# A hybrid decoder block: mixers over pieces of 1,024 tokens, the input projection's feature tiles as seven-product pairs

## The chip, the cores and the metric

The kernel runs on one core of one Trainium2 chip. The metric is the time of one execution in microseconds (us). Engines are named as in the profile: PE multiplies matrices, PEld loads its weights, DVE is the vector engine, ACT the scalar engine (activations and copies), POOL is GpSimd, and SP issues the DMAs. PE writes into PSUM, which here has eight banks of 128 x 512 floats.

## The reference

One decoder layer on one sequence of 2,048 tokens with a model width of 1,024. What matters of it, per layer:

```
h = rms_norm(x) * (1 + scale) + shift
proj = h @ w_in           # q 512 | k,v 128 each | qm,km,vm,om 512 each | i,f 4 each | ga,gm 1024 each
y_a = sliding_window_attention(rope(q), rope(k), v, sinks)        # window 128
qm, km = silu(causal_conv4(qm, km))
y_m = sigmoid(om) * head_norm(mlstm(qm, km, vm, i, f))            # recurrent over chunks
merged = sigmoid(ga) * (y_a @ w_branch_attn) + sigmoid(gm) * (y_m @ w_branch_mlstm)
x = x + gate * rms_norm(merged @ w_out)
x = x + gate_f * rms_norm((silu(h2 @ w_gate) * (h2 @ w_up)) @ w_down)     # h2 from the new x; width 2816
```

Everything is float32. The kernel reaches float32 accuracy with fp32r matmuls: each operand is split into a rounded part `hi` and the rest `lo`, and a product takes three matmuls, hi x hi, hi x lo and lo x hi (`mm3`).

## The kernel before

**Two phases.** The mixers run over four blocks of 512 tokens, `block(b)`, one after the other. Then the FFN runs over two pieces of 1,024 tokens. A build-time planner lays out the order. `run` goes through a list of `Piece`s (mixers) and `run2` through a list of `Part`s (FFN): each is a weight tile with its split and its matmuls. Work beside them (attention, the mLSTM's chunks, the preparation of the next block's h) is written as generators, which `spawn` puts on a list with a due time; `tick`, called after every three matmuls, lets those that are due go a step, and `finish` drives some to their end. The due times count matmul time, in ns (`L_QK`, `L_KW`, `L_SOFT` and so on). The tile framework then orders the instructions of each engine by a modelled timeline and adds the waits and the buffers' reuse.

**One block.** h (8 tiles of 128 features x 512 tokens, hi and lo) lies in two tiles `hhi` and `hlo`. In this order: q, then k, v and the mLSTM's pre-gates, as token groups (`token_group`: tokens on the partitions, four PSUM banks at once); then attention is spawned (`stage2`) beside vm and the feature tiles of ga; then the feature tiles of qm and km (8) with convolution and SiLU in `evac_qk`, and of om (4); then the mLSTM's four chunks are spawned (`stage4`) beside the attention branch's tiles and the feature tiles of gm; then the mLSTM branch's tiles, and the output matmul with the residual (`residual_out`), beside which the next block's h is prepared (`hprep`).

A feature tile (`feature_tile`) is 128 output features x 512 tokens: 8 x 3 matmuls into one PSUM bank, emptied by its `evac`. Its weights are split once for each tile and block, 128 x 1024 at a time (lines 260 and 261). A block has 28: 8 of qm and km, 4 of om, 8 of ga and 8 of gm. All of a block's results (q, qm, km, vm, om, ga, gm, the branch inputs) stay in SBUF, in a pool of nine 1 MB tiles `big` and smaller ones `tm` and `tx`.

**The FFN's pairs.** Gate and up take two 128-feature tiles, two halves of the contraction and both 512-token halves of a piece as a 2 x 2 by 2 x 2 block product in the Strassen-Winograd form: seven products of 12 matmuls instead of eight. The table `PROD` names the operand of the weights and that of h (11, 21, 22 and the sums T1 to T4, in `HC`). `a_operands` makes the weight sums and splits, 128 x 512 each, four parts ahead; `pair_parts` gives the parts; `combine` adds up the results. Products 0, 2, 4 and 6 accumulate in one PSUM bank X, and what is in it is copied out after 0, 2 and 4:

```
if i == 0:
    R["P1"] = new()
    A.copy(R["P1"], ps)
elif i == 1:
    V.tensor_tensor(R["P1"], ps, R["P1"], op=ALU.add)
    done("11", R["P1"], False)
```

In the FFN X lies in one pool of four banks (`acc`) and the other products in a second pool of four (`mix`).

**Lines named in the prediction.** 205 issues every matmul and 210 every transpose. 1135 and 1136 split a 128 x 512 unit into hi (ACT) and lo (DVE). 1286 to 1288 and 1297 make a pair's weight sums. 1337 to 1351 are in `combine`. 912 to 918 are in `evac_qk`: the first convolution tap, the other three, the sigmoid, and the product. 926 scales om. 852 is attention's exponential, 856 its division on POOL.

## Time and profile before

| | |
|---|---|
| runs before | 2763.06 us median of 3 (2759.21 to 2763.97) |
| profiled execution | span 2761.2 us from the first to the last instruction; its own time outside the span is not shown |
| PE busy, matmuls and transposes | 2703.9 us (98%), 12654 |
| DVE / ACT busy | 1916.1 us (69%) / 1234.1 us (45%) |
| DMA | 402.64 MB, mean 146 GB/s |
| start, to 99.5 us | PE busy 73.09 of 99.50 |
| mixers, 99.5 to 1475 us | PE 1366.96, DVE 953.05, ACT 653.04 of 1375.50 |
| FFN, 1475 us to the end | PE 1263.89, DVE 885.20, ACT 534.26 of 1286.20 |

Busy time is the time in which an engine has at least one instruction under way. Matmuls overlap one another, so PE's busy share says where it stands still and not how fast it goes; the speed is read from how many matmuls start in a stretch. In the rows below, `out<-in` names the tiles an instruction writes and reads, `xN` is a count, and what stands behind the second bar is the engine's idle time just before these instructions and who ended it. The granted clock is the share of full speed that PE was allowed.

### The profile page before, as it was taken

The page shows a single profiled execution, that of the slowest core. Times are in us where ns is not written, and L with a number is a line of the kernel's source. Part 1 is how long each engine was busy: PE and PEld are TensorE (multiplying, and loading weights), DVE is VectorE, ACT ScalarE, POOL GpSimd, SP SyncE. Part 2 cuts the span into 40 slices and gives each one's busy share as a digit, 9 for nine tenths or more (in the row PEclk, how much of TensorE's full clock was granted, in tenths as well). Part 3 has the DMA queues.
Part 4 walks back from the last instruction along what each step waited for, and adds up shares of the span by engine and source line. Part 5 has one row for each costly group of instructions (what it writes and reads, how often), then busy time and mean ns, then how long its engine had stood idle before and what let it go on. Part 6 is the DMA issues. An engine that isn't in the chain of part 4 may idle for free.

```text
span 2761.2 us, 35099 instructions
## 1 busy us (share of the span) xinstructions
PE 2703.9 (98%) x12654; PEld 2198.3 (80%) x12654; DVE 1916.1 (69%) x3802; ACT 1234.1 (45%) x2285; POOL 149.6 (5%) x201
## 2 busy tenths in 40 slices
PE   6999999999999999999999999999999999999998
PEld 4778887788887888868887888887777888888886
DVE  7768667587674866747777777776676767666456
ACT  4543365434554335644363343334554333333444
POOL 2100000001000010110100000000000000000000
PEclk9999999999999999999999999999999999999999
DMA  7233353252442424423356555555676423334566
GB/s 235 89 111 97 101 205 105 80 135 83 167 166 66 136 86 153 167 67 101 94 183 212 174 179 167 176 161 192 207 237 206 133 96 111 98 108 136 185 213 214
DMA packets 280534, 402.64 MB, mean 146 GB/s; under 512 B 19220, under 2 KB 176536, under 8 KB 280360
## 3 DMA queue, kind: packets, MB, share of 16 engines
q1 hardware_dynamic: 280360, 400.40, 45.1%
q8 instruction: 99, 1.62, 0.2%
q14 instruction: 75, 0.61, 0.1%
HBM read 320.62 MB, written 79.73 MB: 145 GB/s over the span
## 4 chain that ended last, share of the span: by engine, by line
PE 52%; DVE 2%; DMA 2%; ACT 1%; issue 0%; POOL 0%; SPq 0%; DVEq 0%; POOLq 0%; ACTq 0%
PE acc L205 32%; PE mix L205 19%; DVE hl L1136 1%; DMA raw<-in_w_ffn_down_dram 1%; PE mix L210 1%; ACT hl L1135 0%; DMA raw<-as_d 0%; ACT big L1237 0%; DMA w<-hc_d 0%; DVE w L1497 0%; DMA raw<-in_w_ffn_gate_dram 0%; DMA ws_d<-big 0%; DVE big L1510 0%; DVE w L1533 0%; DVE w L1538 0%
## 5 line engine op out<-in xcount | busy, mean ns | idle before, releaser
L1135 ACT CAST hl<-raw 128x512 fp32r<-128x512 f32 x564 | 337.6, 621 | 403.2 <-PE mix L205 168.8
L1136 DVE TENSOR_TENSOR hl<-raw,hl 128x512 fp32r<-128x512 f32 x564 | 376.6, 686 | 170.7 <-ACT hl L1135 167.9
L260 ACT CAST whi<-raw 128x1024 fp32r<-128x1024 f32 (+1 forms) x208 | 212.2, 1020 | 499.9 <-PE acc L205 444.6
L261 DVE TENSOR_TENSOR wlo<-raw,whi 128x1024 fp32r<-128x1024 f32 (+1 forms) x208 | 249.0, 1197 | 177.5 <-ACT whi L260 175.2
L205 PE MATMUL acc<-hhi,wlo 128*128 128x512 f32 x896 | 356.9, 398 | 0.0
L205 PE MATMUL acc<-hhi,whi 128*128 128x512 f32 x896 | 353.8, 395 | 0.0
L205 PE MATMUL acc<-hlo,whi 128*128 128x512 f32 x896 | 352.9, 394 | 0.0
L205 PE MATMUL acc<-big,hl 128*128 128x512 f32 x1056 | 254.2, 389 | 0.7 <-ACT w L1343 0.7
L205 PE MATMUL acc<-hl,hl 128*128 128x512 f32 x1008 | 236.9, 393 | 7.2 <-DVE hl L1136 4.7
L205 PEld LDWEIGHTS acc<-big,hl 128*128 128x128 f32 x1056 | 198.0, 188 | 42.4 <-ACT w L1343 1.1
L205 PEld LDWEIGHTS acc<-hl,hl 128*128 128x128 f32 x1008 | 187.0, 188 | 52.9 <-DVE hl L1136 9.8
L205 PEld LDWEIGHTS acc<-hhi,whi 128*128 128x128 f32 x896 | 169.7, 189 | 41.2 <-issue 8.1
L205 PEld LDWEIGHTS acc<-hhi,wlo 128*128 128x128 f32 x896 | 169.5, 189 | 39.4 <-issue 4.1
L205 PEld LDWEIGHTS acc<-hlo,whi 128*128 128x128 f32 x896 | 169.3, 189 | 39.5 <-issue 4.9
L205 PE MATMUL mix<-big,hl 128*128 128x512 f32 x704 | 197.3, 391 | 2.6 <-DVE big L1272 2.6
L205 PE MATMUL mix<-hl,hl 128*128 128x512 f32 x792 | 182.4, 391 | 1.8 <-ACT hl L1135 1.0
L205 PEld LDWEIGHTS mix<-hl,hl 128*128 128x128 f32 x792 | 148.0, 188 | 35.5 <-DVE hl L1136 2.6
L205 PE MATMUL acc<-whi,big 128*128 128x512 f32 x512 | 166.5, 396 | 0.0
L205 PE MATMUL acc<-big,whi 128*128 128x512 f32 x512 | 158.4, 394 | 0.0
L205 PEld LDWEIGHTS mix<-big,hl 128*128 128x128 f32 x704 | 132.5, 189 | 30.5 <-DVE big L1272 3.0
L205 PE MATMUL acc<-whi,hhi 128*128 128x512 f32 (+1 forms) x384 | 133.1, 370 | 12.9 <-ACT hhi L505 9.1
L205 PE MATMUL acc<-wlo,hhi 128*128 128x512 f32 (+1 forms) x384 | 139.4, 367 | 2.1 <-DVE wlo L261 2.1
(336 smaller groups left out, 4725.3 us busy)
## 6 DMA issues: line engine op xcount, KB each, us to landing
raw<-in_w_in_dram SPq DMA_DIRECT2D x76, 1024.0 KB, 5.3
as_d<-w SPq DMA_DIRECT2D x154, 256.0 KB, 2.2
raw<-as_d SPq DMA_DIRECT2D x70, 512.0 KB, 3.7
raw<-in_w_ffn_gate_dram SPq DMA_DIRECT2D x22, 1024.0 KB, 5.5
raw<-in_w_ffn_up_dram SPq DMA_DIRECT2D x22, 1024.0 KB, 6.2
raw<-ws_d SPq DMA_DIRECT2D x40, 512.0 KB, 4.7
tx<-in_w_ada_dram SPq DMA_DIRECT2D x64, 256.0 KB, 3.6
raw<-in_w_out_dram SPq DMA_DIRECT2D x16, 1024.0 KB, 5.2
```

The lines of the kernel that those rows point to most:

```text
L205: T.matmul(o, lhsT=lhsT, rhs=rhs, start=start, stop=stop, skip_group_check=resumed)
L210: T.transpose(o, i, ident[:k, :k])
L260: A.copy(hv, src)
L261: V.tensor_tensor(lv, src, hv.bitcast(F32), op=ALU.subtract)
L1135: A.copy(v(hi), src)
L1136: V.tensor_tensor(v(lo), src, v(hi).bitcast(F32), op=ALU.subtract)
```

## The change

The two 512-token blocks of a 1,024-token piece are worked together (`superblock(sb)`), and the 28 feature tiles of each block become 14 pairs for each piece, with the FFN's `pair_parts`. The order in a piece is: q, k, v and the pre-gates of the first block; its attention is started; vm of both blocks; q, k, v of the second block; its attention is started; then the pairs; the mLSTM's eight chunks are started after the eighth pair; then the outputs of both blocks.

- h of the two blocks and its sums T1 to T4 (`HC`) take up to fourteen `big` tiles (the pool grows from nine to fourteen; `tx` from six to nine). `hprep` of the second block reads the first one's h back from DRAM, makes the four sums and writes them out; `hsums` reads and splits them.
- What a block hands on (q, qm and km, vm, om, the gates, the branch inputs) is written to DRAM and read back where it is used: by attention for each 128 queries, by the mLSTM for each chunk, by the outputs in 1 MB tiles.
- All seven products of these pairs use the four `acc` banks. The side work keeps the `mix` banks.
- Sigmoid is made from tanh in the mixers; the factors of two are folded into the constants. The convolution's first tap and om's scaling move from DVE to ACT. The post-mix gain `gg_m` lies in DRAM.
- `Piece` and `run` go; the mixers use `Part` and `run2`. A constant of the build, the DMA scratch size, is set to 1024.

The core of the diff:

```diff
-    bpool = ctx.enter_context(tc.tile_pool(name="bpool", bufs=9))
+    bpool = ctx.enter_context(tc.tile_pool(name="bpool", bufs=14))
...
+        for k in range(4):
+            v11, v21 = tx([P, 512]), tx([P, 512])
+            nc.sync.dma_start(v11, hv_d[sb][:, k, :])
+            nc.sync.dma_start(v21, hv_d[sb][:, k + 4, :])
+            v12 = one(k)
...
+            V.tensor_tensor(v11, v12, v11, op=ALU.subtract)
+            V.tensor_tensor(v12, v22, v12, op=ALU.subtract)
+            V.tensor_tensor(v22, v22, v11, op=ALU.subtract)
+            V.tensor_tensor(v21, v21, v22, op=ALU.subtract)
+            for i, v in enumerate((v11, v22, v12, v21)):
+                nc.sync.dma_start(ht_d[sb][:, i, k, :], v)
...
+    def hsums(sb, names):
+        for name in names:
+            for k in range(4):
+                v = tx([P, 512])
+                nc.sync.dma_start(v, ht_d[sb][:, int(name[1]) - 1, k, :])
+                split_unit(v, hc_part(name, 0)[:, k, :], hc_part(name, 1)[:, k, :])
+                yield L_HS
...
+            qth, qtl = ld([GQ, P], F32R), ld([GQ, P], F32R)
+            for i, q in enumerate((qth, qtl)):
+                nc.sync.dma_start(q.bitcast(F32), q_d[b][:, i, t, :].rearrange("p (j q) -> p j q", j=GQ))
+            yield 0
...
+            nc.sync.dma_start(km, qk_d[b][:, 1, :, cs])
...
+            nc.sync.dma_start(vc[:, :, :MD], vm_d[b][:, t, :].rearrange("p (h d) -> p h d", h=MH))
+            yield L_LOAD
...
+        def done_qk(p):
+            def done(qd, v, in_psum):
...
+                A.activation(ac, u[:, 0:TB], AF.Identity, scale=col("conv_w", f), bias=col("conv_b", f))
+                for j in range(1, 4):
+                    V.scalar_tensor_tensor(ac, u[:, j:j + TB], col("conv_w", j * 8 + f), ac, op0=ALU.mult, op1=ALU.add)
+                sg = tx([P, TB])
+                A.activation(sg, ac, AF.Tanh, scale=0.5)
+                V.scalar_tensor_tensor(ac, sg, 1.0, ac, op0=ALU.add, op1=ALU.mult)
+                nc.sync.dma_start(qk_d[b][:, f // 4, f % 4, :], ac)
...
+            return pair_parts(w_in, c0 + p * 256, done, new, plain, acc_tile)
...
+        def load_y(b, i0):
             for i in range(2):
-                A.activation(R["ga", i], R["ga", i], AF.Sigmoid)
-            R["ml"] = [spawn(mlstm(), L_ML)]
+                R["y", b, i0 + i] = big([4, TB], F32R)
+                nc.sync.dma_start(R["y", b, i0 + i].bitcast(F32), y_d[b][:, i0 + i, :, :])
...
+        pairs = [("qk", 0), ("om", 0), ("qk", 1), ("om", 1), ("qk", 2), ("ga", 0), ("qk", 3), ("ga", 1),
+                 ("ga", 2), ("ga", 3), ("gm", 0), ("gm", 1), ("gm", 2), ("gm", 3)]
+        for i, (kind, p) in enumerate(pairs):
+            parts = list(in_pair(kind, p))
...
+            if i + 1 == len(pairs):
+                yield from parts[:2]
+                yield lambda: (load_y(b0, 0), load_g(b0, 0))
+                parts = parts[2:]
+            yield from parts
+            if (kind, p) == ("ga", 1):
+                yield lambda: end_attention(b1)
+                yield lambda: spawn(mlstm(), L_ML)
+        yield from outputs(b0)
+        yield from outputs(b1)
```

## The prediction

> **What bounds the kernel now.** I read the page first, then the groups of instructions by line, the chain of waits in order of time, and last the busy time in windows. The page gives the span and the engines:

> ```profile
> span 2761.2 us, 35099 instructions
> PE 2703.9 (98%) x12654; PEld 2198.3 (80%) x12654; DVE 1916.1 (69%) x3802; ACT 1234.1 (45%) x2285; POOL 149.6 (5%) x201
> ```

> The three runs before took 2759.21 to 2763.97 us, median 2763.06. That is 1.9 us above the span of the profiled execution, whose own time outside the span is not shown. I make the sum in the span and add 1.9 at the end. A difference of 0.2% (5.5 us) is about what a measurement of this kernel can tell from none.

> PE is busy for 98%, but matmuls are pipelined: one lasts 395 ns and a new one starts sooner. What a matmul costs is therefore its spacing, and that is in the chain of waits (start, length, engine, count). The first row is the mixer, the second one product of the FFN's seven-product pairs:

> ```profile
> 1233.09 51.68 PE acc L205 x227
> ...
> 1575.40 2.72 PE mix L205 x12
> ```

> 51.68 / 227 = 0.2277 us and 2.72 / 12 = 0.2267 us: the two forms of product run at the same rate. I use 0.2267.

> The windows split the span into start, mixers and FFN (stretch, length, PE, PEld, DVE, ACT, POOL busy with counts, granted clock, DMA share, GB/s). The later rows are a stretch of gate/up pairs, then the first down projection:

> ```profile
> 99.50:1475.00 1375.50, 1366.96 (x6707) 1104.00 (x6706) 953.05 (x2131) 653.04 (x1221) 118.48 (x124) 1.00 0.39 121
> ...
> 1500.00:1850.00 350.00, 350.00 (x1544) 289.19 (x1543) 262.75 (x434) 132.86 (x244) 2.16 (x4) 1.00 0.53 174
> 1900.00:2125.00 225.00, 217.95 (x967) 176.01 (x966) 149.80 (x254) 121.84 (x230) 6.51 (x8) 1.00 0.66 220
> ```

> In the mixers PE stands still for 8.5 of 1375.5 us. So whatever PE no longer has to do there is a gain, as long as nothing else makes it wait. DVE is busy for 69% there, ACT for 47%.

> **What the change removes.** The feature tiles of qm/km, om, ga and gm are these groups (count | busy, mean ns):

> ```profile
> L205 PE MATMUL acc<-hhi,wlo 128*128 128x512 f32 x896 | 356.9, 398 | 0.0
> L205 PE MATMUL acc<-hhi,whi 128*128 128x512 f32 x896 | 353.8, 395 | 0.0
> L205 PE MATMUL acc<-hlo,whi 128*128 128x512 f32 x896 | 352.9, 394 | 0.0
> ```

> 3 x 896 = 2688 matmuls, that is 28 tiles x 24 x 4 blocks. After, there are 14 pairs in each of two pieces of 1,024 tokens, with 7 products of 12 matmuls: 14 x 2 x 84 = 2352. So 336 matmuls go, worth 336 x 0.2267 = 76.2 us, all of it in the stretch where PE is the path. Every other matmul and transpose keeps its count: queries, keys and v are still made block by block, and the branch and output matmuls are as before.

> **What it adds on DVE and ACT.** The FFN's pairs show each operation, and the mixer shows what goes:

> ```profile
> L1136 DVE TENSOR_TENSOR hl<-raw,hl 128x512 fp32r<-128x512 f32 x564 | 376.6, 686 | 170.7 <-ACT hl L1135 167.9
> L1135 ACT CAST hl<-raw 128x512 fp32r<-128x512 f32 x564 | 337.6, 621 | 403.2 <-PE mix L205 168.8 <-PE acc L205 161.9 <-DMA raw<-as_d 30.1
> L1287 DVE TENSOR_TENSOR raw<-raw 128x512 f32<-128x512 f32 x44 | 29.9, 680 | 0.0
> L1339 DVE TENSOR_TENSOR w<-mix,w 128x512 f32<-128x512 f32 x44 | 29.9, 680 | 0.1
> L261 DVE TENSOR_TENSOR wlo<-raw,whi 128x1024 fp32r<-128x1024 f32 (+1 forms) x208 | 249.0, 1197 | 177.5 <-ACT whi L260 175.2 <-PE mix L205 1.4
> L260 ACT CAST whi<-raw 128x1024 fp32r<-128x1024 f32 (+1 forms) x208 | 212.2, 1020 | 499.9 <-PE acc L205 444.6 <-issue 52.2 <-DVE big L714 2.8
> L912 DVE TENSOR_SCALAR tx<-tx,cols 128x512 f32<-128x512 f32 x32 | 17.3, 539 | 0.0
> L926 DVE TENSOR_SCALAR big<-big,cols 128x512 f32<-128x512 f32 x16 | 8.8, 547 | 0.2 <-ACT big L925 0.2
> ```

> DVE, for one pair: 7 splits (686 ns), 4 weight sums (680), 4 additions out of PSUM (680) = 10.2 us beside 84 x 0.2267 = 19.0 us of matmuls; 28 pairs make 287 us. Out go 112 splits of 1024 columns, 112 x 1.2 = 134, and the convolution's first tap and om's scaling, which move to ACT: 32 x 0.539 + 16 x 0.547 = 26. In come the sums of h and their splits, 32 x 0.680 + 32 x 0.686 = 44. Net +171 us. DVE in the mixers goes from 953 to about 1124 us, of 1375.5 - 76.2 = 1299: 87%. ACT: 196 x 0.621 - 112 x 1.020 = +7, the new splits of h 32 x 0.621 = 20, the moved scalings 48 at about 0.6 = 29, so 653 + 56 = 709, 55%. The evacuation copies stay at four a pair, and tanh takes sigmoid's place one for one.

> Neither sum is above PE's. I cost this work at nothing in itself, because the gate/up stretch above hides the same pair at DVE 75% (262.75 of 350) with PE at 350.00 of 350. A saturated DVE need not stop PE either. This is the mLSTM of the second block, where DVE worked without a pause:

> ```profile
> 610.00:640.00 30.00, 30.00 (x168) 25.89 (x168) 29.86 (x108) 6.50 (x8) 5.79 (x5) 1.00 0.30 89
> ```

> In the new order the chunks are eight in a row with a planned load time added, beside gate pairs that need only the 10.2 us. The heavier place is the qk pairs: each adds four convolutions on DVE and has attention of the second block beside it.

> **What it adds on the DMA queues.** A block's q, qk, v, om, gates and branch inputs are now written to DRAM and read back: 2 + 2 + 1 + 1 + 4 + 4 = 14 MB, twice, in four blocks 112 MB. The sums of h add 24 and gg_m 2.5; w_in's feature columns (14 MB) are read twice instead of four times, -28. Net +110 MB on 121 GB/s x 1375.5 us = 166 MB, so about 276 MB in 1.3 ms: 211 GB/s and, by the same share per byte, 0.68 of the engines. The first down projection is the nearest row to that (220 GB/s, 0.66, above). Two prices of a transfer (count, KB each, us to landing):

> ```profile
> raw<-in_w_in_dram SPq DMA_DIRECT2D x76, 1024.0 KB, 5.3
> as_d<-w SPq DMA_DIRECT2D x154, 256.0 KB, 2.2
> raw<-as_d SPq DMA_DIRECT2D x70, 512.0 KB, 3.7
> ```

> The tightest load is at the start of the outputs: two branch tiles and two gate tiles of 1 MB are loaded behind the second product of the last pair. The branch tiles land after 2 x 5.3 = 10.6 us and are needed after 5 x 2.72 = 13.6; the gates land at 21.2 and hold PE only when four PSUM banks are full, 13.6 + 4 x 2.72 = 24.5. That is 3.3 us of cover for the tanh of the gates, once for each piece; without cover it is a few us. Attention's query load is followed by its matmuls with no planned delay. Exposed, the 16 loads cost at most 16 x 3.7 = 59 us, hidden nothing. The order of PE's instructions is laid out at build time by modelled readiness, so other matmuls go ahead; I take hidden. All these transfers pass SP, where a write waits for its data, and behind it wait the weight loads, fetched a pair (19 us) ahead.

> **The waits that are new on PE.** A feature tile had four PSUM banks of 5.44 us each to be emptied. A pair accumulates products 0, 2, 4 and 6 in one bank: ACT must copy it before the product after next, one product (2.72 us) later. There are 84 such copies, and behind each waits everything in PE's order. The FFN shows this copy, and 1.0 us of PE's time in which it came late:

> ```profile
> L1337 ACT COPY w<-acc 128x512 f32<-128x512 f32 x44 | 25.6, 581 | 2.0 <-PE acc L205 2.0
> L205 PE MATMUL acc<-hcT2h,hl 128*128 128x512 f32 x352 | 116.0, 390 | 1.0 <-ACT w L1337 1.0
> ```

> A 0.58 us copy in a 2.72 us slot leaves 2.1 us for what ACT has in front of it. Bounds for the stalls: from below nothing (the gate/up row, PE 350.00 of 350), a little less if the waits around attention become fewer. From above the down row, where splits came late at 5.00 of 5 us of DVE:

> ```profile
> 1970.00:1975.00 5.00, 4.00 (x17) 2.85 (x16) 5.00 (x9) 4.77 (x10) 0.00 (x0) 1.00 0.87 235
> ```

> There PE lost 225 - 217.95 = 7.05 us, 3.1%. On the pairs and the attention and mLSTM beside them (28 x 19.0 us, plus about 200 us of side work: estimated) that is 0.031 x 732 = 23 us; on the whole mixer 0.031 x 1299 = 40 us. I take 23, because ACT and DMA come near that row only in these stages.

> A stall can cost more than itself. In the stretch from 460 to 470 us, beside attention and with DVE nearly full, PE lost 1.62 us and the granted clock fell afterwards:

> ```profile
> 460.00:470.00 10.00, 8.38 (x36) 6.52 (x35) 8.85 (x25) 2.58 (x8) 1.78 (x1) 0.83 0.25 63
> 464.00:466.00 2.00, 1.95 (x7) 1.73 (x8) 1.94 (x8) 0.00 (x0) 0.00 (x0) 0.57 0.00 0
> 466.00:468.00 2.00, 2.00 (x7) 1.53 (x6) 2.00 (x7) 0.00 (x0) 0.00 (x0) 0.58 0.27 32
> ```

> 14 matmuls in 4 us instead of 17.6: 0.8 us more, so such a stall costs some 2.4. [...]

> **The sum.** 2761.2 - 76.2 + 23 = 2708.0 us of span, and 1.9 more as a time: 2710 us.

> **The rivals.** First, the pairs run clean, as in gate/up: 2761.2 - 76.2 + 1.9 = 2687. For it speaks PE's 30.00 of 30 under a full DVE; against it, DVE at 87% over all and only four banks for a pair that in the FFN has eight.

> Second, contention over the whole mixer: 40 us instead of 23, and the query loads half exposed (30): 2757 at worst, 2727 without them. For it speaks the DMA share of 0.68; against it, that the loads are mostly placed far ahead.

> Third, slower: ACT stands still for the convolution. Its tanh waits for DVE's three taps, and the copy of the shared bank stands behind that tanh. The chain is these rows:

> ```profile
> L914 DVE SCALAR_TENSOR_TENSOR tx<-tx,cols,tx 128x512 f32<-128x512 f32 x96 | 72.0, 750 | 2.7
> L918 DVE SCALAR_TENSOR_TENSOR big<-tx,tx 128x512 f32<-128x512 f32 x32 | 21.9, 684 | 0.0
> L916 ACT ACTIVATE tx<-tx 128x512 f32<-128x512 f32 x32 | 20.1, 627 | 0.0
> ```

> Two outputs finish at the same product, so a tanh can stand behind a whole chain of 3 x 0.750 + 0.684 = 2.93 us. If each of the 32 outputs holds PE so long, that is 94 us: 2761.2 - 76.2 + 94 + 1.9 = 2781. It decides from 76.2 / 32 = 2.4 us an output. Against it: this tanh's sigmoid never made ACT idle before (0.0 in L916's row), as the order is laid out to fill such gaps. For it: the gaps were then filled under a DVE at 69%. [...]

> That the saving fails to appear as fewer matmuls I exclude: the counts are fixed in the program.

> **Chances.** The forecast 0.40, clean 0.19, contention 0.19, the convolution's chain 0.19, and 0.03 that stalls just cancel the saving. So faster 0.78, same 0.03, slower 0.19. The range runs from 2681 (clean, with the existing 8.5 us of idle mostly gone) to 2768 (contention at its worst with a few us more); it leaves out the chain.

> **What would show it.** PE should have 12318 matmuls, 84 in 19.0 us in a gate pair. DVE should read some 85% in the mixers, ACT 55%, DMA 0.68. PE's idle time in the mixers should be 20 to 35 us, mainly in the qk pairs, its releasers ACT's copies and splits. I am wrong if PE's idle time exceeds 76 us, if its wait is on a DMA rather than on ACT or DVE, or if the stretch before 100 us or the FFN changes by more than 5 us.

## The result, and the profile after

The kernel after took 2799.03 us (median of four runs, 2796.49 to 2799.59), the kernel before 2761.14 us beside it (four runs, 2759.02 to 2763.97). The ratio is 1.0133, with a 95% interval from 1.0118 to 1.0147. The change makes the kernel 38 us slower, where 51 us less was forecast.

The page of the kernel after begins:

```profile
span 2797.0 us, 35939 instructions
...
PE 2662.1 (95%) x12318; PEld 2153.6 (77%) x12318; DVE 2049.0 (73%) x4063; ACT 1259.2 (45%) x2430; POOL 161.7 (6%) x201
```

The matmuls fell to 12318, as counted in advance. Yet PE's busy time fell by only 41.8 us and the span grew by 35.8. To see where, I cut both traces into windows (stretch, length, PE, PEld, DVE, ACT, POOL busy with counts, granted clock, DMA share, GB/s). First the mixers of the kernel before, up to 2 us ahead of the FFN's first copy out of PSUM (in the kernel after, 3 us):

```profile
62.00:1469.00 1407.00, 1396.62 (x6912) 1129.81 (x6911) 979.67 (x2220) 671.26 (x1256) 118.85 (x127) 1.00 0.39 120
```

Then the kernel after, by stage. The first three rows are the first piece: q, k, v and vm; the four qk pairs with om, ga 0 and ga 1 among them, attention beside them; the other gate pairs with the mLSTM, and the outputs. The next three are the second piece, then come the FFN and the mixers as a whole:

```profile
62.00:231.00 169.00, 144.89 (x757) 112.62 (x756) 129.57 (x326) 86.70 (x211) 14.02 (x17) 0.92 0.62 202
231.00:430.00 199.00, 180.14 (x812) 136.75 (x811) 162.58 (x351) 99.53 (x223) 13.40 (x10) 0.97 0.37 119
430.00:790.00 360.00, 358.42 (x1751) 301.43 (x1750) 267.03 (x591) 172.19 (x294) 40.57 (x42) 1.00 0.70 235
790.00:948.00 158.00, 138.09 (x761) 108.46 (x761) 120.72 (x304) 81.57 (x202) 14.45 (x16) 0.94 0.64 209
948.00:1140.00 192.00, 174.51 (x787) 131.78 (x784) 158.36 (x328) 94.91 (x214) 11.88 (x10) 0.97 0.37 118
1140.00:1494.00 354.00, 349.01 (x1706) 292.85 (x1705) 271.67 (x593) 156.78 (x250) 36.10 (x33) 0.99 0.73 236
1494.00:2797.00 1303.00, 1277.64 (x5584) 1041.05 (x5582) 891.37 (x1461) 537.91 (x984) 16.02 (x21) 1.00 0.51 167
62.00:1494.00 1432.00, 1345.06 (x6562) 1083.88 (x6561) 1109.92 (x2487) 691.66 (x1392) 130.43 (x127) 0.97 0.60 197
```

PE stands still for 86.9 us of the mixers, where it stood still for 10.4 (1407.00 - 1396.62). Of the 86.9, the two q, k, v stretches have 24.1 + 19.9 = 44.0, the two stretches of qk pairs 18.9 + 17.5 = 36.4, and everything else 1.6 + 5.0. PE's busy time fell by 1396.62 - 1345.06 = 51.6 where the missing matmuls are worth 76.2, so 25 us are missing. Most of them are a lower clock, 0.92 to 0.97 in the four stretches with the idle time. In the trace the clock stands at 0.50 for 78.5 us of the mixers (10.2 before); PE is busy in 48.1 us of these (10.2 before) and loses half of that, 24.0 us (5.1 before). So 19 of the 25 us are the lower clock, and the other 6 are not explained. The mixers' account is -76 for the matmuls, +76 of idle time, +19 of lower clock and +6 open. The FFN counted from its first copy (1471.2 us before, 1497.2 after) takes 10 us more.

What PE waited for in the kernel after (engine, line waited for: us in all, times, longest us):

```profile
PE acc L206 <- ACT tx L751: 30.2, 7, 15.1
PE acc L206 <- ACT tx L1094: 11.5, 4, 4.1
PE acc L206 <- ACT big L521: 8.3, 3, 3.2
...
PE acc L206 <- DVE hl L1315: 7.0, 7, 2.9
PE mix L211 <- POOL tm L928: 6.6, 5, 2.6
PE mix L206 <- DVE big L1395: 6.1, 1, 6.1
...
PE acc L206 <- DVE tm L599: 4.4, 1, 4.4
```

Line 751 is the rotary's copy out of PSUM, line 1094 the copy of a qk pair's last result out of the shared bank. L521, which evacuates h, was there before (9.1 us in L505). So two places are new and large, and they lie in the two kinds of stretch that lost the time. They are not all of it: L751 has 30 of the 44 us in the q, k, v stretches, and L1094 only 11.4 of the 36.4 in the qk stretches, where the rest is spread over the pairs' splits, attention and the mLSTM.

**The first place: q, k, v.** This is the longest stall. ACT's timeline (start, length, engine, line, operation, and in brackets the idle time ahead of it and who ended it):

```profile
815.54 0.76 ACT L523 ACTIVATE tx<-mix,sh,s 128x512 f32<-128x512 f32 x1
823.83 0.27 ACT L751 COPY tx<-acc 128x128 f32<-128x128 f32 x1 [7.52 <-DMA ht_d<-tx]
```

SP's queue in the same stretch:

```profile
815.15 8.35 SPq L545 DMA_DIRECT2D ht_d<-tx x8
```

This row merges eight issues of 0.32 to 0.87 us, 3.3 us in all; between them SP waits, and at the end for sums that DVE makes late, because what it reads is late:

```profile
819.77 0.69 DVE L540 TENSOR_TENSOR tx<-tx,tx 128x512 f32<-128x512 f32 x1 [1.76 <-DMA tx<-hv_d]
```

The rotary's copy needs a free `tx` tile. Before the change it wrote a `tm` tile; now it shares nine `tx` tiles with `hprep`, which forms the sums of h in four of them at a time and holds them until they are written to DRAM. Reads and writes stand in a burst there:

```profile
806.00:812.00 6.00, 1.38 (x11) 0.84 (x9) 4.22 (x14) 5.98 (x12) 0.00 (x0) 0.77 1.05 399
812.00:818.00 6.00, 0.00 (x0) 0.00 (x0) 5.13 (x14) 4.27 (x6) 0.00 (x0) 0.50 1.02 351
818.00:824.00 6.00, 0.00 (x0) 0.00 (x0) 3.65 (x7) 0.17 (x1) 0.00 (x0) 0.50 1.05 383
824.00:828.00 4.00, 3.86 (x9) 3.12 (x10) 2.96 (x17) 0.89 (x4) 1.21 (x4) 0.50 0.66 250
```

The DMA share is over 1.0 for 18 us, at 350 to 400 GB/s, in a stage whose mean is 0.64. PE's own timeline shows what followed:

```profile
824.14 0.80 PE L206 MATMUL acc<-whi,big 128*128 128x512 f32 x1 [15.11 <-ACT tx L751]
```

It stood still for 15.1 us and then ran at half clock until 829.7 us: 9 matmuls in the 4 us from 824, where 17.6 go at full speed.

**The second place: the qk pairs.** ACT's timeline at one of the four waits:

```profile
334.02 0.63 ACT L1104 ACTIVATE tx<-tx 128x512 f32<-128x512 f32 x1 [1.42 <-DVE tx L1102]
334.56 0.57 ACT L1094 COPY tx<-acc 128x512 f32<-128x512 f32 x1
```

DVE's timeline ahead of it:

```profile
331.11 1.54 DVE L1102 SCALAR_TENSOR_TENSOR tx<-tx,cols,tx 128x512 f32<-128x512 f32 x2
332.64 0.69 DVE L1315 TENSOR_TENSOR hl<-raw,hl 128x512 fp32r<-128x512 f32 x1
333.25 0.74 DVE L1102 SCALAR_TENSOR_TENSOR tx<-tx,cols,tx 128x512 f32<-128x512 f32 x1
```

And PE's:

```profile
335.18 12.13 PE L206 MATMUL acc<-big,hl 128*128 128x512 f32 x45 [3.29 <-ACT tx L1094]
```

DVE makes the three taps with a split between them; ACT's tanh (L1104) waits for the third; the copy of the shared bank stands behind the tanh and starts only 0.54 us after it; PE waits for the copy. That is the third rival's chain, link by link, at this one place. All 32 tanh operations together, in the groups by line (count | busy, mean ns | idle before, releaser):

```profile
L1104 ACT ACTIVATE tx<-tx 128x512 f32<-128x512 f32 x32 | 20.2, 630 | 26.3 <-DVE tx L1102 26.2
```

26.2 us of ACT's idle time, where the same row of the kernel before (L916) had 0.0.

### The profile page after: what moved, and what is told of

The parts are those of the page before. It is cut to its first block, busy times and chain, and to the rows that moved or that the text cites. A ratio compares the mean times of both kernels' runs of the same rounds, so it can differ in the third digit from the quotient of the medians.

```text
span 2797.0 us, 35939 instructions
## 1 busy us (share of the span) xinstructions
PE 2662.1 (95%) x12318; PEld 2153.6 (77%) x12318; DVE 2049.0 (73%) x4063; ACT 1259.2 (45%) x2430; POOL 161.7 (6%) x201
## 4 chain that ended last, share of the span: by engine, by line
PE 78%; DVE 10%; DMA 7%; ACT 2%; issue 1%; SPq 0%; POOL 0%; DVEq 0%; POOLq 0%; ACTq 0%
PE acc L206 55%; PE mix L206 21%; DVE hl L1315 2%; PE mix L211 2%; DMA tx<-in_w_ada_dram 1%; DVE tx L1102 1%; DMA raw<-in_w_ffn_down_dram 1%; ACT hl L1314 1%; DMA ht_d<-tx 1%; DVE tm L431 1%; DMA raw<-as_d 1%; DMA q_d<-tx 1%; DMA tx<-in_g_post_ffn_dram 0%; DVE wlo L262 0%; DMA raw<-in_w_in_dram 0%
## 5 line engine op out<-in xcount | busy, mean ns | idle before, releaser
L206 PE MATMUL acc<-big,hl 128*128 128x512 f32 x3936 | 949.8, 396 | 24.0 <-ACT tx L1094 11.5
L206 PEld LDWEIGHTS acc<-big,hl 128*128 128x128 f32 x3936 | 737.8, 190 | 190.0 <-ACT tx L1094 13.2
L206 PE MATMUL acc<-whi,big 128*128 128x512 f32 (+1 forms) x1280 | 387.5, 382 | 39.4 <-ACT tx L751 30.2
L206 PE MATMUL mix<-big,hl 128*128 128x512 f32 x1232 | 332.9, 391 | 7.3 <-DVE big L1395 6.1
L206 PEld LDWEIGHTS acc<-whi,big 128*128 128x128 f32 x1280 | 237.4, 193 | 90.0 <-ACT tx L751 32.5
L206 PE MATMUL acc<-wlo,big 128*128 128x512 f32 (+1 forms) x640 | 242.3, 380 | 0.4 <-DVE wlo L262 0.4
L261 ACT CAST whi<-raw 128x1024 fp32r<-128x1024 f32 (+1 forms) x96 | 94.3, 982 | 131.7 <-PE acc L206 118.4
L262 DVE TENSOR_TENSOR wlo<-raw,whi 128x1024 fp32r<-128x1024 f32 (+1 forms) x96 | 109.7, 1145 | 58.8 <-ACT whi L261 54.2
L206 PEld LDWEIGHTS acc<-wlo,big 128*128 128x128 f32 x640 | 124.1, 194 | 23.9 <-issue 2.4
L206 PE MATMUL acc<-hcT2h,hl 128*128 128x512 f32 x352 | 118.1, 396 | 1.1 <-ACT w L1458 1.0
## 6 DMA issues: line engine op xcount, KB each, us to landing
raw<-in_w_in_dram SPq DMA_DIRECT2D x48, 1024.0 KB
as_d<-w SPq DMA_DIRECT2D x154, 256.0 KB
raw<-as_d SPq DMA_DIRECT2D x70, 512.0 KB
raw<-in_w_ffn_gate_dram SPq DMA_DIRECT2D x22, 1024.0 KB
raw<-in_w_ffn_up_dram SPq DMA_DIRECT2D x22, 1024.0 KB
raw<-ws_d SPq DMA_DIRECT2D x40, 512.0 KB
tx<-in_w_ada_dram SPq DMA_DIRECT2D x64, 256.0 KB
y_d<-tm SPq DMA_DIRECT2D x64, 256.0 KB
```

Source lines behind the costliest of these rows:

```text
L206: T.matmul(o, lhsT=lhsT, rhs=rhs, start=start, stop=stop, skip_group_check=resumed)
L261: A.copy(hv, src)
L262: V.tensor_tensor(lv, src, hv.bitcast(F32), op=ALU.subtract)
```

## The experiments

Theory 1: the rotary's copies wait for `tx` tiles. Theory 2: the tanh waits for DVE with the copy behind it; its rival is that attention beside the qk pairs is the load (theory 3). Each kernel is the one after with the edit shown. One run each unless said otherwise; the kernel before took 2762.6 us beside e1 to e4, 2761.4 beside e5 to e8 and 2762.5 (seven runs) beside e9 and e10. Runs of the same kernel differ by 3 us in the four of the kernel after, and by up to 7 in the four of e10; the 6 and 7 us of e2 and e4, one run each, are at the edge of that. The idle time of "the qk stretches" below is counted from the first to the ninth copy of a first product (L1458 of the kernel after) in each piece: 37.0 us in the kernel after.

**e1, the rotary's tiles back in `tm`.**

```diff
-            raw = tx([P, W])
+            raw = tm([P, W])
...
-            y = tx([P, W])
-            z = tx([P, W])
+            y = tm([P, W])
+            z = tm([P, W])
```

> The rotary's three tiles a group (raw, y, z) go back from the tx buffers to the tm buffers, where they were before the change; nothing else. Theory 1 (in the q/k/v stretch at the start of each piece PE stops because the rotary's first copy waits for one of nine tx buffers that the preparation of h holds until its sums are written): the 30 us of PE's wait on that copy fall to under 8, and the time falls by 20 to 45 us, to 2755-2780. Rival 1 (ACT and DVE are simply too full there, whichever buffers are used): the wait stays above 20 us or turns up under another name, and the time stays within 8 us of 2799.

2772.99 us, 26 less than the kernel after. PE's waits:

```profile
PE acc L206 <- ACT tm L751: 11.1, 7, 5.0
...
PE acc L206 <- ACT tx L1094: 9.3, 4, 3.3
```

The rotary's wait falls from 30.2 to 11.1 us, and the first pair starts at 226.0 us instead of 233.6; in the second piece it starts at 920.5 instead of 943.6. The wait at L1094 is hardly touched. Theory 1 holds, for 19 us of waits and 7 more that go with them, the lower clock among them; the wait did not fall under the 8 us that were expected. The qk stretches keep 35.5 us of idle time.

**e2, `hprep` of the second block 15 us later.**

```diff
-L_LOAD, L_HP2, L_HC = 4000.0, 1000.0, 3000.0
+L_LOAD, L_HP2, L_HC = 4000.0, 16000.0, 3000.0
```

> The preparation of the second block's h starts 15 us later in the planner's time (L_HP2 16000 for 1000), so that less of it lies beside the rotary of the first block; nothing else. Theory 1: less competition for the tx buffers, the wait on the rotary's copy falls by half or more and the time by 10 to 30 us. Rival 1: the same work is packed into a shorter stretch, the time stays within 8 us or rises.

2792.62 us, 6 less: the wait fell as theory 1 has it, the time only as rival 1 has it. PE's waits:

```profile
PE mix L211 <- POOL tm L928: 19.2, 9, 5.1
PE acc L206 <- ACT tx L751: 10.6, 5, 3.7
```

The rotary's wait falls as far as in e1, but attention's division on POOL now holds PE for 19.2 us instead of 6.6. Moving the competitor in time moves the stall with it; another pool removed it.

**e3, the convolution without its three taps on DVE.** The first tap alone remains.

```diff
-                for j in range(1, 4):
+                for j in range(1, 1):
```

> Leaves out the convolution's three taps on DVE (96 instructions of 0.75 us), so the outputs are not the reference's. Theory 2 (in the qk pairs ACT's tanh waits for these taps, and PE for the bank copies behind it): the waits of PE in the stretches of the qk pairs, some 36 us of idle time before, fall by more than half, and the time by 20 to 40 us. Rival 2 (it is attention's exponentials, 4.6 us at a time on ACT, that hold the copies): the idle time there stays above 25 us and the time falls by under 12.

2751.85 us, 47 less. In the groups by line the pairs' matmuls, which waited 24.0 us after the change (11.5 of it for L1094), now read:

```profile
L206 PE MATMUL acc<-big,hl 128*128 128x512 f32 x3936 | 943.7, 394 | 6.4 <-DVE hl L1315 4.1 <-ACT tx L1094 1.8 <-ACT hl L1314 0.5
```

Attention is still there and the qk pairs hardly wait (5.9 us of idle time in the qk stretches): theory 2 and not theory 3. The 47 us are an upper bound for the wait, since 96 taps of 0.776 us, 74.5 us of DVE's work, are gone as well. The rotary's wait is 30.2 us as before, so the two places are independent.

**e4, another order:** the four ga pairs first, beside attention; then qk and om; the mLSTM after the last qk pair.

```diff
+        pairs = [("ga", 0), ("ga", 1), ("ga", 2), ("ga", 3), ("qk", 0), ("om", 0), ("qk", 1), ("om", 1),
+                 ("qk", 2), ("gm", 0), ("qk", 3), ("gm", 1), ("gm", 2), ("gm", 3)]
```

> The order of the pairs alone: the four ga pairs first, beside the second block's attention, then the qk and om pairs; the mLSTM starts after the last qk pair, two pairs later than before. Theory 2: attention and the convolution no longer meet, so PE's idle time in the pairs falls from some 36 us to under 15 and the time by 15 to 35 us. Rival 2 (attention's exponentials alone): the stalls move with attention into the ga pairs and the time stays within 8 us. A third way: the mLSTM, started later, ends later and PE waits for it before the first block's second branch, which adds 10 us or more.

2792.24 us, 7 less. PE's waits:

```profile
PE acc L206 <- ACT tx L1094: 8.0, 4, 2.1
PE acc L206 <- DMA big<-y_d: 7.5, 1, 7.5
PE acc L206 <- ACT tx L1459: 7.4, 5, 1.7
```

Without attention beside them the qk pairs still wait for L1094, and now for the next pair's copy too (L1459 is L1458 of the kernel after). That speaks against theory 3 a second time, but theory 2's own numbers, under 15 us of idle time in the pairs and 15 to 35 us of time, were missed too. A new wait for the branch inputs, read right after they are written, takes part of the gain back.

**e5, the sums of h not written to DRAM.** `hsums` reads other rows of h instead, so half of the pairs' operands hold other values, while every later instruction stays.

```diff
-                nc.sync.dma_start(ht_d[sb][:, i, k, :], v)
+                pass
...
-                nc.sync.dma_start(v, ht_d[sb][:, int(name[1]) - 1, k, :])
+                nc.sync.dma_start(v, hv_d[sb][:, 2 * k + int(name[1]) % 2, :])
```

> Leaves out the 32 writes of the sums T1 to T4 of h to DRAM (the sums are still made; their splits read the first block's h instead, so the outputs are not the reference's). Theory 1 (rotary tiles wait for tx buffers that these writes hold): PE's wait on the rotary's copy falls from 30 us to under 12 and the time by 15 to 35 us from 2799. Rival 1 (any tenant of tx would do, or the engines are too full): the wait stays above 20 us, the time within 8 us.

2782.45 us, 17 less. PE's wait for the rotary:

```profile
PE acc L206 <- ACT tx L751: 21.6, 6, 7.5
```

The longest wait halves and the sum falls by 8.6 us. The time falls as theory 1 has it, while the wait stays above the 20 us of rival 1. The writes are a part of it, with 8 MB less for the DMA besides; that the `tx` tiles held by `hprep`'s additions and by q's own write are the rest, which e1 reached and this did not, is argued and not shown.

**e6, tanh, product and write in a stream of their own**, planned 5 us later. All work stays; only ACT no longer meets the tanh ahead of the copy.

```diff
+L_SILU = 5000.0
...
-                sg = tx([P, TB])
-                A.activation(sg, ac, AF.Tanh, scale=0.5)
-                V.scalar_tensor_tensor(ac, sg, 1.0, ac, op0=ALU.add, op1=ALU.mult)
-                nc.sync.dma_start(qk_d[b][:, f // 4, f % 4, :], ac)
+                def silu():
+                    yield L_SILU
+                    sg = tx([P, TB])
+                    A.activation(sg, ac, AF.Tanh, scale=0.5)
+                    V.scalar_tensor_tensor(ac, sg, 1.0, ac, op0=ALU.add, op1=ALU.mult)
+                    nc.sync.dma_start(qk_d[b][:, f // 4, f % 4, :], ac)
+                g = silu()
+                R.setdefault("silu", []).append(spawn(g, next(g)))
...
+                yield lambda: finish(R["silu"])
```

> All work kept: in the qk pairs the tanh, the product and the write come 5 us later in the planner's time, in a stream of their own, so that ACT should not meet the tanh before DVE has done the taps. Theory 2a (what costs is ACT standing in order behind the taps): PE's waits on the copies in the qk pairs fall as without the taps, and the time by 20 to 40 us from 2799. Theory 2b (what costs is DVE's load of 72 us of taps itself, whose splits and additions come late): the time falls by under 12 us. A third way: the tx buffers, held longer, make new waits, and the time rises.

2767.61 us, 31 less. The tanh is now L1107, in the groups by line:

```profile
L1107 ACT ACTIVATE tx<-tx 128x512 f32<-128x512 f32 x32 | 19.7, 627 | 9.0 <-DVE tx L1103 6.9 <-DVE hl L1321 2.0
```

The qk stretches, as windows:

```profile
234.56:427.57 193.01, 185.82 (x841) 141.52 (x838) 161.73 (x335) 101.26 (x229) 13.69 (x8) 0.98 0.38 120
932.15:1127.68 195.53, 187.76 (x854) 144.79 (x852) 168.24 (x351) 102.86 (x231) 12.03 (x10) 0.97 0.40 128
```

ACT's wait for the taps falls from 26.2 to 6.9 us with DVE's work the same, the copy of the last result is no longer among PE's waits, and the idle time of the qk stretches falls from 37.0 to 7.2 + 7.8 = 15.0 us. This is theory 2 by its order alone: DVE's load was not the trouble, the place of the waiting instruction was. (The product on DVE and the write move with the tanh; that it is ACT's queue and not theirs rests on the rows at 334 us.)

**e7, e1 and e6 together.**

> The rotary's tiles in tm and the later tanh together. If the two places are independent, the gains add: 2773 less the gain of the later tanh alone (20 to 40 us by theory 2a, that is 2733-2753, under the kernel before; by theory 2b 2761-2773).

2733.92 us, 65 less than the kernel after: 26 + 31 and 8 more. **e9** is the same kernel timed in five rounds.

> Both moves at once (rotary's tiles in the other pool; tanh, product and write of a convolution in a stream of their own, planned 5 us later), timed in five rounds. One look gave 2734. If the rotary's buffers and the tanh are the two places in which the change's saving went, the kernel is faster than the one before by 25 to 30 us: a ratio of 0.989 to 0.991. If that look was a chance one, the ratio is nearer to 1.

2735.44 us (four runs, 2733.62 to 2738.47), a ratio to the kernel before of 0.9907 with an interval from 0.9891 to 0.9924: faster than both kernels. PE's longest waits of it:

```profile
PE acc L207 <- ACT tm L752: 10.3, 7, 5.0
PE acc L207 <- ACT hl L1320: 9.1, 5, 6.0
PE acc L207 <- ACT big L522: 8.1, 3, 3.2
...
PE acc L207 <- ACT tx L1464: 6.9, 2, 5.9
```

**e8, the gate pairs as plain feature tiles** on the kernel after: seven of a piece's eight, 168 matmuls more.

```diff
+            if kind[0] == "g" and (kind, p) != ("gm", 3):
+                return plain_tiles(kind, p, c0 + p * 256)
```

> Undoes 7 of the 8 gate pairs of a piece: two feature tiles for both blocks instead, 96 matmuls for 84 (the operand 12 is not in SBUF there, 11 stands in for it, so the gates of every second block are not the reference's). The saving's own term: 7 x 12 x 2 = 168 more matmuls at 0.2267 us, 38 us more, 2837, if these pairs run on PE's path without waits. If instead the gate pairs were held by DVE or ACT, the plain tiles, lighter on DVE, would cost under 20 us more.

2818.02 us, 19 more, half of what the count gives, as the second case has it. The windows of its qk stretches and of its mixers say why:

```profile
231.00:430.00 199.00, 187.13 (x838) 142.79 (x837) 147.96 (x306) 96.22 (x214) 13.30 (x10) 0.97 0.36 117
...
957.00:1160.00 203.00, 192.28 (x862) 146.06 (x861) 154.66 (x314) 97.45 (x215) 11.13 (x9) 0.97 0.38 123
...
62.00:1512.00 1450.00, 1379.61 (x6734) 1113.65 (x6733) 1023.20 (x2307) 665.53 (x1322) 128.07 (x127) 0.97 0.60 194
```

PE's busy time rises by 34.6 us, but its idle time falls from 86.9 to 70.4, most of it (14 us) in the windows of the qk pairs, where ga 0 and ga 1 lie. A plain tile has no bank that must be copied within one product, which fits.

**e10, the same edit on e9's kernel**, four runs. In e8 and e10 the second block's gates read the first block's h in half of their contraction; the instructions are those of full feature tiles.

> The same kernel as e9 with seven of a piece's eight gate pairs written as plain feature tiles again (14 pairs in the two pieces, 14 x 12 = 168 matmuls more). It asks what the pairs save where nothing waits. If the gate pairs bring their full count, it is 168 x 0.2267 = 38 us slower than e9: about 2772. If pairs hand back a part as stalls of their own (as the one look on the changed kernel, +19, could mean), it is 15 to 22 us slower: about 2752. In the first case the +19 came from waits beside the two earliest gate pairs, which the moved tanh has taken away.

2780.14 us (four runs, 2778.81 to 2785.57), 44.7 more than e9 on the same chip. The mixers of e9:

```profile
62.00:1445.00 1383.00, 1338.30 (x6587) 1079.33 (x6585) 1108.55 (x2497) 692.58 (x1399) 130.72 (x128) 0.99 0.63 204
```

and of e10:

```profile
62.00:1485.00 1423.00, 1376.23 (x6744) 1110.17 (x6742) 1020.38 (x2312) 664.04 (x1326) 127.26 (x128) 0.99 0.61 198
```

The two windows do not end alike: e9's runs 3.8 us into the FFN, e10's 0.2. Both cut at the FFN's first copy (1441.2 and 1484.8 us), e10 has 41.0 us more of PE's busy time, where the count gives 38.1, and 46.6 against 44.0 us of idle time. So a gate pair keeps its full saving there. The time goes 6.6 us beyond the count, as much as e10's runs differ among themselves. Between the profiled runs, of which e10's is its slowest, it is 51.2 us, 43.6 in the mixers and 7.5 in the FFN; why the FFN differs is not known.

## Why the prediction was wrong

**What held.** 336 matmuls went, at 0.2267 us each: e10 gives half of them back for 41.0 us of busy time, 38.1 by the count. The gate pairs run clean as in gate/up (358.42 of 360 us in the first piece, 349.01 of 354 in the second). The added work was no larger than forecast: the durations of DVE's instructions ahead of the FFN add up to 164 us more (171 forecast; its busy time rises by 130, as instructions overlap), ACT's to 32 more (56 forecast), and the kernel moves 116 MB more (110 forecast). Neither the query loads nor the gate loads at the outputs appear among PE's longest waits.

**What failed: the stall term.** It was 23 us and measured 76.5, with 25 more of PE's busy time, 19 of it the lower clock, and 10 at the FFN. Three of the signs named in advance showed: over 76 us of idle time, the FFN, and the start (PE busy in 62.23 of the first 99.5 us, 73.09 before). The failure has four parts.

- *The base.* The 3.1% was laid on the pairs and the side work beside them. 44.0 of the 86.9 us of idle time lie ahead of the pairs, in q, k, v and vm, where I costed nothing. I had counted `hprep`'s sums as DVE's and DMA's work, but not as holders of `tx` tiles, and passed over the rotary's three tiles, which the diff moves from `tm` to `tx`. e1 undoes those three lines and takes 26 us off.
- *The rate.* In the qk stretches PE stood still for 36.4 of 391 us, 9.3%, not 3.1%. The rate came from a stage where splits came late, a different wait. What held PE here was for the larger part the tanh's place ahead of the copies (e6 takes 22 of 37 us away), and no busy share of another stage measures that.
- *The clock.* I showed that a stall of 1.62 us cost some 2.4 and then left the factor out of the sum. The factor was too small besides: 4 of the 14 matmuls that I counted there are short transposes. In windows of 1 us from 464 on the clock reads 0.64, 0.50, 0.50 and 0.65, which is 1.7 us of work lost, so that stall cost 3.3. In the result the lower clock is 19 us on 76.5. The record changes in steps of 3.41 us. Each of its twelve falls in the mixers of the kernel after came at the end of a step in which PE had stood still for 1.7 us or more, in pieces or at once; the three of the kernel before followed 1.3 to 1.6 us. In the longest stall the clock fell right at the start (PE had stopped at 809.0):

```profile
809.00:810.00 1.00, 0.03 (x1) 0.00 (x0) 0.47 (x2) 1.00 (x4) 0.00 (x0) 0.61 1.06 406
```

In the 3.41 us ahead of that fall PE had stood still for 1.84 us in all.

- *The FFN.* I expected less than 5 us of change there and it took 10 more. At its start PE waits 6.1 us for L1395, which makes the FFN's operands of h after a read from DRAM, where the kernel before waited 2.6, and in the FFN's first 26 us the two kernels issue 71 and 87 matmuls: 16 x 0.2267 = 3.6 us. Most of the other 6 us are the products with T2 and T4, whose matmuls follow one another in 0.233 us where they took 0.227. In the prediction's row of T2 they last 390 ns; here:

```profile
L206 PE MATMUL acc<-hcT2h,hl 128*128 128x512 f32 x352 | 118.1, 396 | 1.1 <-ACT w L1458 1.0
```

The FFN's T4 row goes from 389 to 395 ns and the second T2 row (`hcT2l`) too; with 880 matmuls in the three rows that is 5 us. The traces of e1 to e3 and e5 to e9 have 396 or 397 ns in the `hcT2h` row too, and why is not known.

**The third rival** had the mechanism of the second place, and a chance of 0.19. My argument against it was the 0.0 us in the sigmoid's row of the kernel before. That row told only of DVE as it was then: from the start of a convolution's first tap to the end of its last the kernel before took 2.9 us (median of 32), and the sigmoid started 0.6 us later. In the kernel after the same chain takes 4.3 us, up to 11.4, with splits and other work between the taps, and 16 of the 32 tanh operations wait for its end. That the copy stands behind the tanh in ACT's order, which this rival needs, no row of the kernel before had shown. The rows at 334 us show it: the copy starts 0.54 us after a tanh that had waited 1.42 us for the taps. The rival's own price was too high, though: 94 us, against the 31 us that e6 takes off and the 47 of e3 with the taps' work gone. Nor is the result, 2799, above its 2781 us by this chain alone: with the first place undone (e1) the kernel takes 2773 us, 10 more than the kernel before beside it, and the first place was in none of the cases. So no case was the true one: two mechanisms of about equal size added up, and one of them was not on the list.

**Contention** was named as the DMA's share, 0.68 forecast over the mixers, 0.60 measured. The mean was the wrong number: for 18 us the share was above 1.0, and there the longest wait lies.

**What stays open.** e9 still has 44.7 us of idle time in the mixers where the kernel before had 10.4. Of these, 21 us lie ahead of the first piece's pairs, about as many as in the kernel after (24), so e1's gain is mostly in the second piece. The largest waits of e9 are at the rotary's copy, the first split of a pair and a bank copy, at 6 to 10 us each. The 6 to 8 us (e9 and e7) that e1 and e6 give together beyond their sum lie in the FFN: counted to its first copy, the mixers are 23.5 us shorter in e1, 31.5 in e6 and 56.0 in e9, which adds up, while the FFN behind it takes 1299.8 us after the change, 1297.6 in e1, 1300.2 in e6 and 1291.5 in e9. They lie in its first 60 us, where e9 issues 254 matmuls and the kernel after 220 (34 x 0.2267 = 7.7 us); the wait for the FFN's operands of h, 6.1 us after the change, 2.7 in e1 and 7.1 in e6, is not among e9's. Why both edits are needed for that is not known.

## What to carry to other kernels

Moving a step changes what it holds, not only what it does: list, for each pool, who takes a tile and which event gives it back, because a pool shared with a burst of DMA writes can turn those writes into a wait of whoever needs the next tile, as here for the rotary's copy (30.2 us of PE's waits, 11.1 with the other pool). When a bank must be emptied within one product, look along the copying engine's queue for an instruction that waits for a third engine; planning that instruction later (e6) kept all the work and took 31 us off, and removing the tile conflict (e1) took 26; with both, the change was faster than the kernel before, by 0.9%. A mean share of busy time or of DMA showed neither here (the DMA's mean was 0.60 over the mixers and its share above 1.0 for 18 us): price a stall in its own stage, and add what the clock takes afterwards (here 19 us beside 76.5).

## What the runs showed of the hardware that was not expected

Matmuls of one shape did not all follow one another at the same rate: in the FFN those with T2 and T4 took 0.233 us each after the change and 0.227 before it, with the clock at 1.00 and no wait between them.
